# One layer of a hybrid encoder on one core: sums of squares used two products later, two operand pools of the second stage in the other order, and the second stage's last block with fewer merges and one PSUM tile for each last result

## The chip, the cores and the metric

The kernel runs on one core of one Trainium2 chip. The metric is the device time of one execution in microseconds. The five engines each work through their own queue in order: TensorE (PE, matrix products into PSUM), VectorE (DVE), ScalarE (ACT), GpSimd (POOL) and SyncE (SP, which here only issues transfers). ACT issues some transfers too. Shown below are the kernel's times in plain runs and one execution taken by the hardware profiler.

## The reference, cut to what matters

For one batch of 1024 positions of width 1024:

- `u = RMSNorm(x)`, one projection `u @ w_in`, then two mixers side by side: banded attention in chunks of 64, and a gated delta-rule recurrence in chunks.
- `h = x + concat[RMSNorm(attention), delta] @ w_out`
- `h = h + relu(RMSNorm(h) @ w_ff1)^2 @ w_ff2`, with `w_ff1` 1024 x 4096 and `w_ff2` 4096 x 1024, all float32.

The change lies in the last line alone. RMSNorm divides each position by the root of the mean of its squares over 1024 channels; the kernel multiplies the gain in first, squares after the relu, and so needs `1/mean(h*h)` (no root) as a factor on the squared result, one number for each position.

## The kernel before, in words

Everything is kept transposed: channels on the 128 partitions, positions along the free axis, in two halves of 512. A float32 product is made from three float32r products (high x high, high x low, low x high), so each operand is split on the way: ACT copies it to the high part (line 146), DVE subtracts that from it to get the low part (line 147). A page is a 128 x 1024 float32 tile, 4 KB in each partition.

**Stage 1 (`ff1`, lines 987 to 1132)** computes the first product in 8 blocks of 512 hidden channels. Each block is one step of a fast matrix multiplication with 7 products instead of 8, named q1, q2, q5, q6, q3, q7, q4 in the order of the code, of 24 matmuls each. Their position-side operands (b11, b21, t1, t2, b22, t3, t4: quarters of `h` or differences of them) are split once, by `uop`, in the first block and stay in their pools (`ub11` ... `ut4`, four pages each) for all blocks. The four results of a block are z11 (from q1 and q2), z12, y5 and y1; each goes through relu and square on ACT (`square`) and through `emit`, in which DVE multiplies by the factor row `r2` and ACT's queue stores it to `f_dr`.

The factor comes from the sums of squares that the stage before left in `sq_dr`. `norm_col` (1025) loads them into a page `acc`, has PE add them up over the partitions (`hcol`, 16 small matmuls), and DVE makes `r_col` of it. `norm_row` (1035) has PE spread that over all partitions (`hrow`), and ACT copies it to `r2`. Blocks are generators that stop at `yield`; lines 1125 to 1132 step them: q1 of block 0 and of block 1, then `norm_col`; q2 of both, then `norm_row`; then the rest of block 0, of block 1, and the other blocks. z11, z12 of blocks 0 and 1 and `acc` are pages of pool `ut4`, in which the four pages of operand t4 lie too; later blocks use other space (`zz`).

**Stage 2 (`ff2`, 1134 to 1292)** multiplies by `w_ff2` in 4 blocks (`kb` 0 to 3) of 1024 hidden channels, again by 7 products a block, p1, p2, p5, p3, p6, p7, p4, of 48 matmuls. `product` (1150) takes two PSUM tiles of two banks out of the four of pool `psw`, and prepares operand pairs 0 and 1 in turn by `prep5`, `prep3`, ... (sums and differences on DVE, in place) and by splitting. Operands are loaded at the top of a block: a11 and b11 into pool `r`, a12, b21 and b22 into pool `r2`, a21, a22 and b12 into pool `rc`. `accumulate` adds a product to one of the pages y1 to y7 (DVE, one input from PSUM). In the last block `merge` adds one y to another (both inputs in SBUF), on POOL (`nc.gpsimd`) or DVE (`nc.vector`), so that y2, y3, y5 and y4 become the four quarters of the output, which `store` and the last loop write out. The last product, p4, is made row by row (`by_rows`): quarter q of the result is complete before the next begins, and is subtracted into y4 and sent at once.

**What sets the order.** The code's order is only a priority. A planner walks a simulated timeline before the program runs and writes each engine's queue from it; on the chip the queue is then run in that order, whatever the real times. A tile's space is reused in its pool when its last user is done. Stage 2's pools (line 1308) are laid out from the same base as stage 1's (1306), one behind the other in the order of the dictionary, so a page of stage 2 waits for the page of stage 1 that lay there.

Of the kernel before, what the change touches and what calls it, by code (L numbers as in the profile page):

```python
# [8 lines left out]
F32 = mybir.dt.float32  # L9
# [36 lines left out]
def hymba_kernel(  # L46
# [940 lines left out]
    def ff1(R, psw, pools):  # L987
# [2 lines left out]
        B = {}  # L990
        count = [0]
        r2 = pools["r2"][0].tile([P, 2, TH], F32, tag="r2", name="r2", bufs=1)
        begun = {}

        def page2(tag, name, dt=F32):
            pool, n = pools[tag]
# [46 lines left out]
        def block(sb):  # L1043
            def lw(tag, name, kh, c):
                t = page2(tag, f"{name}_{sb}")
                c0 = sb * FB + c * 256
                nc.sync.dma_start(out=t.rearrange("p (k c) -> p k c", k=4),
                                  in_=w_ff1[kh * 512:(kh + 1) * 512, c0:c0 + 256].rearrange("(k p) c -> p k c", p=P))
                return t

            first = "w" if sb else "w0"
            a11 = lw(first, "wa11", 0, 0)
            a12 = lw(first, "wa12", 1, 0)
            if sb > 1:
                a21, a22 = lw("w", "wa21", 0, 1), lw("w", "wa22", 1, 1)
            yy = quarter(f"yy{sb}")
            y1, y5 = wide(yy, 0), wide(yy, 1)

            def product(name, src, key):
                n = f"{name}_{sb}"  # L1060
                ps = psw.tile([P, 1024], F32, tag="bk", name=n)
                ah, al = parts(src, n + "a", key)
                if key in LAST:
                    hi, lo = begun[LAST[key]]
                    with tc.issue_after(hi), tc.issue_after(lo):
                        bop = uop(key)
                else:
                    bop = uop(key)
                for k in range(4):
                    bh, bl = bop[k]  # L1070
                    for q in range(2):
                        s = slice(k * 256 + q * P, k * 256 + (q + 1) * P)
                        for m, (l, r) in enumerate(((ah, bh), (ah, bl), (al, bh))):
                            nc.tensor.matmul(part(ps, q), l[:, s], r, start=(k + m == 0), stop=(k == 3 and m == 2))  # L1074
                return ps

            def square(t):
                nc.scalar.activation(t, t, AF.Relu)
                nc.scalar.activation(t, t, AF.Square)

            def emit(t, fh, th):
                nc.vector.tensor_tensor(two(t), two(t), r2[:, th:th + 1, :].broadcast_to([P, 2, TH]), ALU.mult)
                nc.scalar.dma_start(out=f_dr[sb * 4 + fh * 2:sb * 4 + fh * 2 + 2, :, th * TH:(th + 1) * TH].rearrange(
                    "q p t -> p q t"), in_=two(t))

            ps = product("q1", a11, "b11")
            nc.scalar.copy(y1, ps)
            yield
            ps = product("q2", a12, "b21")
            zz = None  # L1090
            if sb > 1:
                zz = quarter(f"zz{sb}")
            z11 = wide(zz, 0) if zz is not None else page2("ut4", f"z11_{sb}")
            nc.vector.tensor_tensor(z11, y1, ps, ALU.add)
            square(z11)
            yield
            emit(z11, 0, 0)
            if sb <= 1:
                a21, a22 = lw("w", "wa21", 0, 1), lw("w", "wa22", 1, 1)
            s1 = page2("w", f"ws1_{sb}")  # L1100
            nc.vector.tensor_tensor(s1, a21, a22, ALU.add)
            ps = product("q5", s1, "t1")
            nc.scalar.copy(y5, ps)
            nc.vector.tensor_tensor(s1, s1, a11, ALU.subtract)
            ps = product("q6", s1, "t2")
            nc.vector.tensor_tensor(y1, y1, ps, ALU.add)
            nc.vector.tensor_tensor(y5, y5, y1, ALU.add)
            nc.vector.tensor_tensor(a12, a12, s1, ALU.subtract)
            ps = product("q3", a12, "b22")
            z12 = wide(zz, 1) if zz is not None else page2("ut4", f"z12_{sb}")  # L1110
            nc.vector.tensor_tensor(z12, y5, ps, ALU.add)
            square(z12)
            emit(z12, 0, 1)
            nc.vector.tensor_tensor(a21, a11, a21, ALU.subtract)
            ps = product("q7", a21, "t3")
            nc.vector.tensor_tensor(y1, y1, ps, ALU.add)
            nc.vector.tensor_tensor(y5, y5, ps, ALU.add)
            square(y5)
            emit(y5, 1, 1)
            ps = product("q4", a22, "t4")  # L1120
            nc.vector.tensor_tensor(y1, y1, ps, ALU.subtract)
            square(y1)
            emit(y1, 1, 0)

        first = [block(sb) for sb in range(2)]
        for i in range(2):
            for g in first:
                next(g)
            (norm_row if i else norm_col)()
        for g in first + [block(sb) for sb in range(2, DFF // FB)]:  # L1130
            for _ in g:
                pass
# [1 line left out]
    def ff2(psw, pools):  # L1134
# [15 lines left out]
        def product(name, prep, by_rows=False):  # L1150
            t = "AB"[side[0]]
            side[0] ^= 1
            ps = [psw.tile([P, 1024], F32, tag="bk", name=f"{name}{m}") for m in range(2)]
            def step(i, k, q):
                (ah, al), (bh, bl) = ops[i]
                s = slice(k * 512 + q * P, k * 512 + (q + 1) * P)
                for m, (l, r) in enumerate(((ah, bh), (ah, bl), (al, bh))):
                    nc.tensor.matmul(part(ps[q // 2], q % 2), l[:, s], part(r, k),  # L1158
                                     start=(i + k + m == 0), stop=(i + k + m == 4))

            ops = []
            for i in range(2):
                ab = []
                for o, src in zip("ab", prep(i)):
                    hi = page2("h" + t, f"{name}{o}{i}_h", F32R)
                    lo = page2("l" + t, f"{name}{o}{i}_l", F32R)
                    split(src, hi, lo, nc.scalar, nc.vector)
                    ab.append((hi, lo))
                ops.append(ab)
                if not by_rows:  # L1170
                    for k in range(2):
                        for q in range(4):
                            step(i, k, q)
            if by_rows:
                for q in range(4):
                    for i in range(2):
                        for k in range(2):
                            step(i, k, q)
            return ps

        def store(x, j, hf):
            for m in range(2):
                nc.sync.dma_start(out=out[0, (4 * j + 2 * m) * P:(4 * j + 2 * m + 2) * P, hf * TH:(hf + 1) * TH].rearrange(
                    "(q p) t -> p q t", p=P), in_=two(x[m]))

        nb = DFF // (2 * NK * P)
        for kb in range(nb):
# [69 lines left out]
            if last:  # L1257
                merge(nc.gpsimd, 2, 1)
                store(y[2], 0, 0)
                merge(nc.gpsimd, 6, 1)  # L1260
            accumulate(5, product(f"p5{kb}", prep5))
            if last:
                merge(nc.gpsimd, 3, 5)
                for m in range(2):
                    nc.gpsimd.tensor_tensor(y[5][m], y[5][m], h11[m], ALU.add)
            accumulate(3, product(f"p3{kb}", prep3))
            ps = product(f"p6{kb}", prep6)
            if last:
                merge(nc.vector, 7, 6)
                merge(nc.vector, 3, 6)  # L1270
                accumulate(3, ps)
                store(y[3], 0, 1)
                accumulate(7, ps)
                merge(nc.vector, 4, 7)
                merge(nc.gpsimd, 5, 7)
            else:
                accumulate(6, ps)
            ps = product(f"p7{kb}", prep7)
            if last:
                accumulate(4, ps)  # L1280
                accumulate(5, ps)
                store(y[5], 1, 1)
            else:
                accumulate(7, ps)
            ps = product(f"p4{kb}", prep4, last)
            if not last:
                accumulate(4, ps, ALU.subtract)
                continue
            for q in range(4):
                t = part(y[4][q // 2], q % 2)  # L1290
                tt(t, t, part(ps[q // 2], q % 2), ALU.subtract)
                (nc.scalar if q % 2 else nc.sync).dma_start(out=out[0, (4 + q) * P:(5 + q) * P, 0:TH], in_=t)

    def ffn(R):
        with ExitStack() as st:
# [9 lines left out]
            with ExitStack() as st1:  # L1305
                ff1(R, psw, stage(st1, "ff1", {"w0": 2, "h": 2, "l": 2, "ub11": 4, "ub21": 4, "ut1": 4, "ut2": 4,
                                               "ub22": 4, "ut3": 4, "ut4": 4, "w": 6, "h2": 1, "l2": 1, "r2": 1}))
            ff2(psw, stage(st, "ff2", {"s1": 2, "hB": 4, "r": 8, "hA": 4, "lA": 4, "rc": 6, "r2": 8, "lB": 4, "y7": 2}))

    def first_steps(gen, n):  # L1310
        for _ in range(n):
# [77 lines left out]
```

## Time and profile before

| | us |
|---|---|
| median of 3 runs | 1318.98 |
| lowest and highest of them | 1316.98, 1319.04 |
| the profiled execution, whole | 1311.28 |
| its span, first to last instruction | 1309.2 |
| PE busy in it | 1267.2 (97%) |
| DVE busy | 937.3 (72%) |
| ACT busy | 554.3 (42%) |
| POOL busy | 306.0 (23%) |

The profiled execution is 7.7 us shorter than the median of the plain runs. Stage 1 runs from 670 to 984 us of the span, stage 2 from 984 to the end. A busy PE counts matmuls whose ends are modelled, and says nothing of the clock that they ran at; the granted clock stands in a row of its own on the page and in a column of the views by stretches.

### The profile page before, as it was taken

To read this page: it belongs to the slowest core of one execution; us is meant where nothing else is said; L and a number is where in the kernel's file an instruction comes from. 1 tells how busy PE (TensorE), PEld (TensorE's weight loads), DVE (VectorE), ACT (ScalarE), POOL (GpSimd) and SP (SyncE) were. 2 spreads that over 40 slices of the span, in tenths; PEclk is the share of its full clock that TensorE was granted. 3 is DMA by queue.
4 is the path that set the end of the run, shared out by engine and by line. 5 is a ranking of instruction groups with operands and counts; after the bars stand their busy time and mean duration, and the time that the engine had idled before them with its cause. 6 is when DMAs were issued, how large, how long until landed. Compare 5 with 4: busy or idle time off the path is not lost.

```text
span 1309.2 us, 18076 instructions
## 1 busy us (share of the span) xinstructions
PE 1267.2 (97%) x6702; PEld 1044.5 (80%) x6702; DVE 937.3 (72%) x1395; ACT 554.3 (42%) x919; POOL 306.0 (23%) x509
## 2 busy tenths in 40 slices
PE   9999999999999998989999999999998999999997
PEld 7778878788888877868878888888886888888876
DVE  7899978655056565853539767677669878897998
ACT  7323232223266564744345444544445543333330
POOL 4426451543033365533210000000000000000251
PEclk9999999999999999989999999999998999999999
DMA  6214354665573532124341323323288514332002
GB/s 219 65 49 141 95 151 129 137 161 145 197 223 105 166 96 74 53 62 157 129 145 65 113 97 113 129 97 113 80 294 300 181 52 153 98 97 97 1 33 97
DMA packets 129256, 160.65 MB, mean 123 GB/s; under 512 B 22800, under 2 KB 71952, under 8 KB 128656
## 3 DMA queue, kind: packets, MB, share of 16 engines
q1 hardware_dynamic: 111328, 137.73, 34.1%
q10 hardware_dynamic: 17840, 21.76, 4.8%
q8 instruction: 53, 0.87, 0.3%
q14 instruction: 35, 0.29, 0.1%
HBM read 111.75 MB, written 47.71 MB: 122 GB/s over the span
## 4 chain that ended last, share of the span: by engine, by line
PE 73%; DVE 8%; DMA 3%; ACT 2%; POOL 1%; issue 1%; SPq 0%; DVEq 0%; ACTq 0%; POOLq 0%
PE q L1074 23%; PE p L1158 19%; PE op L165 5%; PE av_ps L165 3%; PE aq_ps L165 3%; PE t_o L858 3%; PE g_ps L165 3%; PE ak_ps L165 2%; DVE y L1223 1%; PE t_tpb L837 1%; PE t_tpa L848 1%; PE t_sb L785 1%; PE t_sa L785 1%; DMA t_q<-q_dr 1%; PE t_sb L786 1%
## 5 line engine op out<-in xcount | busy, mean ns | idle before, releaser
L1227 POOL TENSOR_TENSOR y<-y,y 128x1024 f32<-128x1024 f32 x8 | 24.7, 3111 | 587.7 <-DVE y L1223 587.7
L801 DVE CUSTOM_DVE_ANT_0 t_pb<-t_sb,biasn 128x256 f32<-128x256 f32 (+1 forms) x64 | 25.7, 403 | 55.5 <-PE t_sb L786 30.3
L1223 DVE TENSOR_TENSOR y<-y,p 128x1024 f32<-128x1024 f32 x50 | 59.9, 1216 | 5.3 <-PE p L1158 4.4
L165 PE MATMUL op<-mh,wo_h 128*128 128x512 f32 x128 | 50.3, 393 | 0.8 <-ACT wo_h L146 0.5
L165 PE MATMUL op<-ml,wo_h 128*128 128x512 f32 x128 | 50.1, 391 | 0.0
L165 PE MATMUL op<-mh,wo_l 128*128 128x512 f32 x128 | 48.3, 392 | 0.0
L816 ACT ACTIVATE t_pb<-t_pb,t_nm 128x256 f32<-128x256 f32 (+1 forms) x64 | 31.6, 494 | 22.8 <-DVE t_nm L810 15.0
L955 DVE TENSOR_TENSOR h<-op,op_x 128x512 f32<-128x512 f32 x16 | 10.8, 688 | 31.9 <-PE op L165 31.9
L858 PE MATMUL t_o<-t_ta,vt 128*64 128x128 f32 x240 | 29.0, 294 | 1.8 <-DVE t_ta L851 1.1
L962 POOL TENSOR_TENSOR op_q<-op_q 128x512 f32<-128x512 f32 x14 | 19.6, 1397 | 47.5 <-ACT op_q L961 47.3
L810 DVE CUSTOM_DVE_ANT_0 t_pa<-t_sa,biaso,t_nm 128x384 f32<-128x384 f32 (+2 forms) x48 | 26.3, 548 | 5.5 <-PE t_sa L786 3.3
L165 PEld LDWEIGHTS op<-mh,wo_h 128*128 128x128 f32 x128 | 24.0, 188 | 7.0 <-ACT wo_h L146 1.0
L165 PEld LDWEIGHTS op<-mh,wo_l 128*128 128x128 f32 x128 | 24.0, 188 | 5.2 <-issue 0.2
L165 PEld LDWEIGHTS op<-ml,wo_h 128*128 128x128 f32 x128 | 24.0, 188 | 5.0
L819 ACT ACTIVATE t_pa<-t_pa,t_nm 128x384 f32<-128x384 f32 (+2 forms) x48 | 26.4, 550 | 0.1
L165 PE MATMUL g_ps<-uh,wg_h 128*128 128x512 f32 x64 | 25.2, 394 | 1.2 <-ACT wg_h L146 1.2
L848 PE MATMUL t_tpa<-ident,t_pa 128*128 128x128 f32 x120 | 21.7, 285 | 4.5 <-ACT t_on L886 3.2
L785 PE MATMUL t_sb<-ks,t_q 128*128 128x256 f32 (+1 forms) x72 | 23.2, 333 | 2.9 <-DMA t_q<-q_dr 2.9
L165 PE MATMUL g_ps<-uh,wg_l 128*128 128x512 f32 x64 | 25.2, 394 | 0.4 <-POOL wg_l L147 0.4
L165 PE MATMUL dq_ps<-uh,wdq_h 128*128 128x512 f32 x64 | 25.5, 398 | 0.0
L165 PE MATMUL dv_ps<-uh,wdv_l 128*128 128x512 f32 x64 | 25.4, 397 | 0.0
L165 PE MATMUL aq_ps<-waq_h,uh 128*128 128x512 f32 x64 | 25.3, 401 | 0.0
(1106 smaller groups left out, 4418.4 us busy)
## 6 DMA issues: line engine op xcount, KB each, us to landing
wa<-in_w_ff_dram SPq DMA_DIRECT2D x32, 512.0 KB
a<-in_w_ff_dram SPq DMA_DIRECT2D x32, 512.0 KB
b<-f_dr SPq DMA_DIRECT2D x32, 512.0 KB
t_q<-q_dr SPq DMA_DIRECT2D x32, 256.0 KB
f_dr<-yy ACTq DMA_DIRECT2D x16, 512.0 KB
f_dr<-zz ACTq DMA_DIRECT2D x12, 512.0 KB
ks<-k_dr SPq DMA_DIRECT2D x16, 256.0 KB
wo_r<-in_w_out_dram SPq DMA_DIRECT2D x16, 256.0 KB
```

The source lines that it names most:

```text
L165: nc.tensor.matmul(ps, a, b, start=(i == 0), stop=(i == n - 1))
L785: nc.tensor.matmul(o, q[:, i * P:(i + 1) * P], k[:, c], start=True, stop=False)
L801: nc.vector.tensor_tensor_reduce(sb[:, c], bk[:, c], new[g][pp][:, c], -1.0, 3.0e38, ALU.add, ALU.min, nm[:, 4 + i:5 + i])
L810: nc.vector.tensor_tensor_reduce(sa[e][:, 0:wa], bk[:, 0:wa], old[g][i][:, 384 - wa:384], -1.0, nm[:, 4 + i:5 + i], ALU.add, ALU.min, nm[: ...
L816: nc.scalar.activation(sb[:, c], sb[:, c], AF.Exp, bias=m, scale=-1.0, accum_out=T["sums"][:, 4 + i:5 + i])
L819: nc.scalar.activation(sa[e][:, 0:wa], sa[e][:, 0:wa], AF.Exp, bias=m, scale=-1.0, accum_out=T["sums"][:, i:i + 1])
L848: nc.tensor.transpose(tp[:, js], sa[e][:, js], ident)
L858: nc.tensor.matmul(po[64 * e:64 * e + 64, pp * P:(pp + 1) * P], vt[k0 + j][:, 64 * h:64 * h + 64], (ta[e] if j < na else tb)[:, c:c + P], ...
L1074: nc.tensor.matmul(part(ps, q), l[:, s], r, start=(k + m == 0), stop=(k == 3 and m == 2))
L1158: nc.tensor.matmul(part(ps[q // 2], q % 2), l[:, s], part(r, k), start=(i + k + m == 0), stop=(i + k + m == 4))
L1223: nc.vector.tensor_tensor(y[i][m], y[i][m], ps[m], op)
L1227: eng.tensor_tensor(y[i][m], y[i][m], y[z][m], ALU.add)
```

## The change

It has four parts. (1) In stage 1 the generators of the first two blocks are stepped through q1 and q2 of both before `norm_col`, then block 0 through q5 and q6 before `norm_row`; `emit` of z11 of blocks 0 and 1 is put behind `norm_row`. Two `yield`s are added for it. (2) In the dictionary of stage 2's pools `r2` and `rc` change places. (3) In the last block the merge of y1 into y6 goes from POOL to DVE and behind p6, p6 is added to y6 alone and p7 to y7 alone, each then merged on, and y5 gets its last part by a POOL merge; its store goes to ACT's queue. (4) p4 in the last block gets four PSUM tiles, one for each quarter, and its four last transfers all go to SP.

```diff
@@ ff1
-        begun = {}
+        begun, held = {}, []
...
             square(z11)
+            if sb <= 1:
+                held.append((emit, z11))
             yield
-            emit(z11, 0, 0)
             if sb <= 1:
                 a21, a22 = lw("w", "wa21", 0, 1), lw("w", "wa22", 1, 1)
             s1 = page2("w", f"ws1_{sb}")
             nc.vector.tensor_tensor(s1, a21, a22, ALU.add)
             ps = product("q5", s1, "t1")
             nc.scalar.copy(y5, ps)
+            yield
+            if sb > 1:
+                emit(z11, 0, 0)
             nc.vector.tensor_tensor(s1, s1, a11, ALU.subtract)
             ps = product("q6", s1, "t2")
             nc.vector.tensor_tensor(y1, y1, ps, ALU.add)
             nc.vector.tensor_tensor(y5, y5, y1, ALU.add)
+            yield
...
         for i in range(2):
             for g in first:
                 next(g)
-            (norm_row if i else norm_col)()
+        norm_col()
+        for _ in range(2):
+            next(first[0])
+        norm_row()
+        for emit, z in held:
+            emit(z, 0, 0)
@@ ff2, product and store
-            ps = [psw.tile([P, 1024], F32, tag="bk", name=f"{name}{m}") for m in range(2)]
+            ps = [psw.tile([P, 1024], F32, tag="bk", name=f"{name}{m}") for m in range(4 if by_rows else 2)]
...
-                    nc.tensor.matmul(part(ps[q // 2], q % 2), l[:, s], part(r, k),
+                    nc.tensor.matmul(part(ps[q], 0) if by_rows else part(ps[q // 2], q % 2), l[:, s], part(r, k),
...
-        def store(x, j, hf):
+        def store(x, j, hf, eng=nc.sync):
             for m in range(2):
-                nc.sync.dma_start(
+                eng.dma_start(
@@ ff2, the blocks
             if last:
                 merge(nc.gpsimd, 2, 1)
                 store(y[2], 0, 0)
-                merge(nc.gpsimd, 6, 1)
             accumulate(5, product(f"p5{kb}", prep5))
+            accumulate(3, product(f"p3{kb}", prep3))
+            accumulate(6, product(f"p6{kb}", prep6))
             if last:
+                merge(nc.vector, 6, 1)
                 merge(nc.gpsimd, 3, 5)
                 for m in range(2):
                     nc.gpsimd.tensor_tensor(y[5][m], y[5][m], h11[m], ALU.add)
-            accumulate(3, product(f"p3{kb}", prep3))
-            ps = product(f"p6{kb}", prep6)
+                merge(nc.vector, 3, 6)
+                store(y[3], 0, 1)
+            accumulate(7, product(f"p7{kb}", prep7))
             if last:
                 merge(nc.vector, 7, 6)
-                merge(nc.vector, 3, 6)
-                accumulate(3, ps)
-                store(y[3], 0, 1)
-                accumulate(7, ps)
                 merge(nc.vector, 4, 7)
                 merge(nc.gpsimd, 5, 7)
-            else:
-                accumulate(6, ps)
-            ps = product(f"p7{kb}", prep7)
-            if last:
-                accumulate(4, ps)
-                accumulate(5, ps)
-                store(y[5], 1, 1)
-            else:
-                accumulate(7, ps)
+                store(y[5], 1, 1, nc.scalar)
             ps = product(f"p4{kb}", prep4, last)
             if not last:
                 accumulate(4, ps, ALU.subtract)
                 continue
             for q in range(4):
                 t = part(y[4][q // 2], q % 2)
-                tt(t, t, part(ps[q // 2], q % 2), ALU.subtract)
-                (nc.scalar if q % 2 else nc.sync).dma_start(out=out[0, (4 + q) * P:(5 + q) * P, 0:TH], in_=t)
+                tt(t, t, part(ps[q], 0), ALU.subtract)
+                nc.sync.dma_start(out=out[0, (4 + q) * P:(5 + q) * P, 0:TH], in_=t)
@@ ffn
-  {"s1": 2, "hB": 4, "r": 8, "hA": 4, "lA": 4, "rc": 6, "r2": 8, "lB": 4, "y7": 2}
+  {"s1": 2, "hB": 4, "r": 8, "hA": 4, "lA": 4, "r2": 8, "rc": 6, "lB": 4, "y7": 2}
```

## Rows read from the trace of the kernel before

**Rows 1.** The page: busy time of the engines over the whole span, and the chain that ended last by engine.

```profile
PE 1267.2 (97%) x6702; PEld 1044.5 (80%) x6702; DVE 937.3 (72%) x1395; ACT 554.3 (42%) x919; POOL 306.0 (23%) x509
...
PE 73%; DVE 8%; DMA 3%; ACT 2%; POOL 1%; issue 1%; SPq 0%; DVEq 0%; ACTq 0%; POOLq 0%
```

**Rows 2.** Who waited for whom, PE alone, whole span: us in total, times, the longest; the rows of stages 1 and 2.

```profile
PE p L1158 <- ACT p20b_h L146: 5.4, 1, 5.4
...
PE p L1158 <- DVE p43b_l L147: 2.5, 1, 2.5
PE hcol L1031 <- DMA acc<-sq_dr: 2.2, 1, 2.2
...
PE p L1158 <- DVE y L1223: 2.0, 1, 2.0
```

**Rows 3.** PE in order of time around `hcol` (start, duration, idle before and its releaser in brackets), and the stretch 685 to 690 us (busy time and instructions of PE, PEld, DVE, ACT, POOL; granted clock; DMA share; GB/s).

```profile
681.91 0.39 PE L1074 MATMUL q<-b11h,q_1a_l 128*128 128x512 f32 x1
684.51 1.92 PE L1031 MATMUL hcol<-ones,acc 128*128 128x1 f32 x16 [2.21 <-DMA acc<-sq_dr]
686.29 0.48 PE L1074 MATMUL q<-b21h,q_0a_h 128*128 128x512 f32 x1
...
690.95 0.40 PE L1074 MATMUL q<-b21l,q_0a_h 128*128 128x512 f32 x1
...
685.00:690.00 5.00, 5.00 (x24) 4.24 (x25) 5.00 (x5) 2.98 (x4) 0.00 (x0) 0.74 0.00 0
```

**Rows 4.** Two stretches with the columns of rows 3: 695 to 700 us, and the last product of the third block of stage 2 (its 48 matmuls and the one under way); and two subtractions of DVE in order of time.

```profile
695.00:700.00 5.00, 5.00 (x29) 4.30 (x28) 5.00 (x6) 3.58 (x4) 0.00 (x0) 1.00 0.07 15
...
1209.13:1220.01 10.88, 10.88 (x49) 9.01 (x48) 10.85 (x10) 4.01 (x5) 0.00 (x0) 1.00 0.00 0
...
700.48 1.23 DVE L147 TENSOR_TENSOR t2l<-h,t2h 128x1024 fp32r<-128x1024 f32 x1
...
720.10 1.22 DVE L147 TENSOR_TENSOR t4l<-h,t4h 128x1024 fp32r<-128x1024 f32 x1
```

**Rows 5.** Where stage 1 ends and stage 2 begins, in order of time on PE, ACT, DVE and SP; one row of SP's waits; the stretch 990 to 1000 us with the columns of rows 3.

```profile
1000.06 1.22 PE L1158 MATMUL p<-p20b_h,p20a_h 128*128 128x512 f32 x2 [5.38 <-ACT p20b_h L146]
...
1004.88 0.39 PE L1158 MATMUL p<-p50b_h,p50a_h 128*128 128x512 f32 x1
...
1000.85 1.06 ACT L146 CAST p20b_h<-b 128x1024 fp32r<-128x1024 f32 x1
...
981.80 1.22 DVE L1111 TENSOR_TENSOR z<-yy,q 128x1024 f32<-128x1024 f32 x1
...
986.38 1.22 DVE L1233 TENSOR_TENSOR s<-a,a 128x1024 f32<-128x1024 f32 x1
...
978.17 1.40 SPq L1193 DMA_DIRECT2D a<-in_w_ff_dram  x3
979.61 1.34 SPq L1193 DMA_DIRECT2D b<-f_dr  x2
...
995.71 0.89 SPq L1193 DMA_DIRECT2D b<-f_dr  x2
...
SPq L1193 <- DMA f_dr<-z: 8.2, 1, 8.2
...
990.00:1000.00 10.00, 4.68 (x21) 3.56 (x19) 10.00 (x9) 7.70 (x9) 0.00 (x0) 0.90 1.03 377
```

**Rows 6.** The last block in order of time: POOL, then DVE, then PE.

```profile
1249.27 5.75 POOL L1227 TENSOR_TENSOR y<-y,y 128x1024 f32<-128x1024 f32 x2 [10.24 <-DVE y L1223]
1260.72 6.63 POOL L1227 TENSOR_TENSOR y<-y,y 128x1024 f32<-128x1024 f32 x2 [5.70 <-DVE y L1223]
1267.31 6.72 POOL L1265 TENSOR_TENSOR y<-y,h 128x1024 f32<-128x1024 f32 x2
1286.60 5.72 POOL L1227 TENSOR_TENSOR y<-y,y 128x1024 f32<-128x1024 f32 x2 [12.56 <-DVE y L1223]
...
1244.57 1.21 DVE L1227 TENSOR_TENSOR y<-y,y 128x1024 f32<-128x1024 f32 x1
...
1250.24 2.51 DVE L1239 TENSOR_TENSOR a<-a,s 128x1024 f32<-128x1024 f32 x1
1252.67 3.44 DVE L1252 TENSOR_TENSOR b<-b,b 128x1024 f32<-128x1024 f32 x1
...
1284.11 4.61 DVE L1223 TENSOR_TENSOR y<-y,p 128x1024 f32<-128x1024 f32 x4
...
1300.11 1.28 DVE L1291 TENSOR_TENSOR y<-y,p 128x512 f32<-128x512 f32 x2
...
1260.70 0.71 PE L1158 MATMUL p<-p63b_h,p63a_h 128*128 128x512 f32 x1 [1.99 <-DVE y L1223]
...
1264.18 0.42 PE L1158 MATMUL p<-p63b_h,p63a_l 128*128 128x512 f32 x1
...
1293.45 0.50 PE L1158 MATMUL p<-p43b_l,p43a_h 128*128 128x512 f32 x1 [2.55 <-DVE p43b_l L147]
...
1298.61 0.40 PE L1158 MATMUL p<-p43b_l,p43a_h 128*128 128x512 f32 x1
```

**Rows 7.** The end: DVE, SP, and the end of the chain that ended last.

```profile
1304.77 1.29 DVE L1291 TENSOR_TENSOR y<-y,p 128x512 f32<-128x512 f32 x2 [3.38 <-PE p L1158]
...
1300.22 0.37 SPq L1183 DMA_DIRECT2D out_dram<-y  x1
```

More of the change, by code (lines that the diff above doesn't have):

```diff
@@ L1179, in product @@
             return ps
-        def store(x, j, hf):
+        def store(x, j, hf, eng=nc.sync):
             for m in range(2):
-                nc.sync.dma_start(out=out[0, (4 * j + 2 * m) * P:(4 * j + 2 * m + 2) * P, hf * TH:(hf + 1) * TH].rearrange(
+                eng.dma_start(out=out[0, (4 * j + 2 * m) * P:(4 * j + 2 * m + 2) * P, hf * TH:(hf + 1) * TH].rearrange(
                     "(q p) t -> p q t", p=P), in_=two(x[m]))
@@ L1307, in ffn @@
                                                "ub22": 4, "ut3": 4, "ut4": 4, "w": 6, "h2": 1, "l2": 1, "r2": 1}))
-            ff2(psw, stage(st, "ff2", {"s1": 2, "hB": 4, "r": 8, "hA": 4, "lA": 4, "rc": 6, "r2": 8, "lB": 4, "y7": 2}))
+            ff2(psw, stage(st, "ff2", {"s1": 2, "hB": 4, "r": 8, "hA": 4, "lA": 4, "r2": 8, "rc": 6, "lB": 4, "y7": 2}))
     def first_steps(gen, n):
```

## The prediction

> **What bounds the kernel now.** First the page: PE is busy for 1267.2 of 1309.2 us, and the chain that ended last runs through PE for 73% of the span [rows 1]. So time is saved where PE waits, or runs at its lower clock after a wait. The second view is who waited for whom, PE alone [rows 2]. Four waits lie where the change reaches: 2.2 us for the sums of squares, 5.4 us at the start of p2 in stage 2, and 2.0 and 2.5 us in the last block. The third is PE in order of time. At full speed 48 matmuls start in 10.88 us, 0.227 us each [rows 4]. After the wait at `hcol`, 13 matmuls take from 686.29 to 690.95, 4.66 us instead of 2.95 (1.7 lost), and the granted clock of the stretch is 0.74, a mean of the levels 1.2 and 2.4 GHz [rows 3]. After the 5.38 us wait 11 matmuls take 1000.06 to 1004.88: 4.82 instead of 2.50, 2.3 lost [rows 5]. In the last block 8 take 1260.70 to 1264.18 (1.7 lost) and 15 take 1293.45 to 1298.61 (1.8 lost) [rows 6]. A wait thus costs its own length and about 2 us more:
>
> - sums of squares 2.2 + 1.7 = 3.9
> - start of p2 5.4 + 2.3 = 7.7
> - last block 2.0 + 1.7 + 2.5 + 1.8 = 8.0
>
> Together 19.6 us; add a short tail behind PE's last matmul.
>
> **Part 1, sums of squares later.** `hcol` waits because `acc` lands at 684.5, while q1 of block 1 has started its last matmul at 681.91 [rows 3]. Put behind the two q2 (2 x 24 x 0.227 = 10.9 us), it comes at 693 and finds `acc` there. The q2 started directly behind `hcol`, so its operands were ready: 2.2 us of waiting go. The 1.7 us of low clock go with them unless `hcol` alone brings it down; `hrow`, 16 matmuls as well, stands in 695 to 700 at a granted 1.00 [rows 4]. Added are no instructions; the two `emit` and the load of `acc` keep their queues. Late next is DVE, which is full: 5.00 of 5.00 us both in 685 to 690 and in 695 to 700 [rows 3, 4]. PE would reach q6 at about 693 + 1.9 + 5.4 = 700.3 and want the second half of t2 2.7 us later, at 703.0; its low part ends at 701.7 now [rows 4], and z11, now ready sooner, goes ahead of it once (1.2 us): 702.9, in time by a hair. Further on t4's first low part ends at 721.3, and PE arrives up to 3.9 us earlier than it did. Bounds: all 3.9 gained if DVE's order gives way, 0.5 if DVE holds PE back for nearly all of it. I take 3.0.
>
> **Part 2, the pools change places.** Counted in pages from the base, stage 1 has ub22 at 22 to 25, ut3 at 26 to 29, ut4 at 30 to 33, then w. `r2` lies on 28 to 35 before and 22 to 29 after, `rc` on 22 to 27 and then 30 to 35. So p2's operands (a12, b21) now wait for t3, t4 and the page that z12 of block 1 took when t4 left it; that sum is made only at 981.80, its store must land, SP waits 8.2 us for that, and the load of b21's last page goes out at 995.71 [rows 5]. Because they come late, ACT's queue has p2's casts behind p5's, and PE waits. After, a12 and b21 lie on pages that are free when q3 and q7 are done, at 978.2 at the latest, which is when `rc`'s loads went out before. Those were in SBUF when DVE added two of them at 986.38 [rows 5]; a cast (1.05) and a subtraction (1.22) later, at 989, p2 could go, and p1 ends at 1000.06 - 5.38 = 994.7. So 7.7 us go. Late next is p5, whose operands take over the pages of t4. The page behind z12's store is free at 995.71; b21's second page, loaded then, was cast at 1000.85, so 5.1 us bound load and queue. A sum (1.22), a cast and a subtraction bring 1004.3; p2 ends at 994.7 + 10.9 = 1005.6. That is 1.3 us of slack, with DVE full (10.00 of 10.00) and the DMA share at 1.03 [rows 5]. Bounds: 7.7 gained, or 1.0 if p5 takes over most of the wait. I take 6.7.
>
> **Parts 3 and 4, the last block.** A two-input operation of DVE on SBUF takes 1.2 us alone and 3.4 beside POOL; one with an input in PSUM keeps 1.15 (4.61 for four, half beside POOL); POOL's take 2.9 to 3.4 each [rows 6]. From 1250.24 to 1301.39 DVE does 32 whole operations and 2 halves in 51.2 us, from the first of the rows with that start to the last [rows 6]: 32 x 1.135 + 1.2 = 37.5 of work, so the eight POOL operations cost it 13.6, or 1.7 each. It is this backlog that makes PE wait both times. The change takes away:
>
> - the POOL pair at 1249.27, which slowed the two operations from 1250.24 to 1256.1: 2 x 1.7 = 3.4;
> - two DVE operations: before 16 accumulations (beside the last four halves) and 6 merges, after 12 and 8: 2 x 1.135 = 2.3. (Two of the merges, y6 into y7, were done by 1245.8 [rows 6] and now come behind p7.)
>
> DVE would come to the second half at 1301.4 - 5.7 = 1295.7; PE without waits ends at 1304.75 - 8.0 = 1296.8. But a chain now begins with p7's end (1296.8 - 10.9 = 1285.9): y7 gets p7 (2), y6 is merged in (2), y4 gets y7 (2), while POOL adds y7 to y5 (2). That is 6 x 1.135 + 2 x 1.7 = 10.2, to 1296.1; then four halves at 0.6, to 1298.5. The last half ended at 1304.77 + 1.29 = 1306.06 [rows 7]: 7.5 gained. The PSUM tile for each quarter frees q2 from waiting for q3 (0.6, inside that sum). Against it, y5's last store went out at 1300.22, 5.8 us before the last half [rows 7]; now its pages come with y4's, 2 MB in the last few us, and the tail of 3.1 us may grow; I take 1.2 of 0 to 2. ACT issues nothing else then, so the queue that the store moves to costs nothing. Gained: 7.5 - 1.2 = 6.3; bounds 8.6 (tail too) and 1.7 (only the wait at p6 goes, 3.7, and y5 is 2 late).
>
> The Trainium skill (SBUF — State Buffer, section Who interferes with whom) says that a VectorE operation with at most one SBUF input does not contend with GpSimd and one with two does, the later of the two being blocked whole. The rows agree. It speaks against this part: p7 went into y4 and y5 by accumulations with one SBUF input, and goes now by two-input merges beside POOL; by the rule alone each of the two merges into y4 waits for a whole POOL operation, some 2 us more than I reckon.
>
> **Sum.** 3.0 + 6.7 + 6.3 = 16.0. From the profiled execution's 1311.3 that makes 1295.3; its median stands 7.7 us higher in the plain runs, and I carry the difference over: 1318.98 - 16.0 = 1303.0.
>
> **The rivals.**
>
> 1. The last block stays bound by what DVE and POOL share: the merges behind p7 keep DVE past PE's end, and only the wait at p6 is won. For it speaks that DVE was busy for 10.85 of 10.88 us already in the product before [rows 4], against it the 5.7 us of work removed. 1318.98 - 3.0 - 6.7 - 1.7 = 1307.6.
> 2. p5 takes the wait over: the page behind z12's store, or the loads behind it in SP's queue, come 5 us late. For it the DMA share of 1.03, against it the 1.3 us of slack and a queue that carries the same bytes. 1318.98 - 3.0 - 1.0 - 6.3 = 1308.7.
> 3. Slower: the planner leaves PE's queue as it is, two matmuls of p2, then 31 of p5 (they run from 1001.08), then the rest of p2. p5's operands are now the late ones. If all six loads go out from 995.7 on at 377 GB/s, 0.52 MB take 1.4 us each and the last is in at 1004; one pair's four operations on DVE and a cast make it 1009.6, and six more of DVE's in front 1016.4. PE then waits 21.7 us and loses 2.3, 24.0 instead of 7.7: 16.3 lost against 9.3 gained elsewhere, 1326. It decides when p5's operands come later than 994.7 + 5.4 + 9.3 = 1009.4. Against it: p2's operands are ready first by 6 us, and the planner goes by that.
> 4. The sums of squares are not used later, because the planner issues `hcol` where it was: part 1 is worth nothing, 1306.
>
> **Chances.** The forecast 0.50, rival 1 0.22, rival 2 0.12, rival 3 0.07, rival 4 0.09. About 0.2%, 2.6 us, is what a measurement of this kernel can tell from no change. Two of rivals 1, 2 and 4 together, with part 1 lost to DVE, would come near no change: 0.06 out of their 0.43. So faster 0.87, same 0.06, slower 0.07. The range goes from 1297 (all upper bounds, 20.2, with 2 us of scatter) to 1313 (rivals 1 and 2 at once: 3.0 + 1.0 + 1.7 = 5.7).
>
> **What would show it.** `hcol` behind two q2, with no wait of PE and a granted clock of 1.0 around it; p1, p2, p5 in this order with less than 1.5 us between them; no wait of PE for an accumulation before p6; POOL with eight operations instead of ten from 1225 on; the last half of y4 some 2 us behind PE's last matmul. A new wait of PE at q6, t4, p5 or p4's second pair would each show one of my terms wrong; one above 5 us would make the prediction wrong.

## The result, and the profile after

| | before | after |
|---|---|---|
| median of 18 plain runs each, on one chip (us) | 1316.69 | 1307.92 |
| the profiled execution, whole (us) | 1311.28 | 1307.01 |
| its span (us) | 1309.2 | 1305.2 |

The ratio is 0.9943 with a 95% interval of 0.9925 to 0.9961: 7.5 us faster (5.1 to 9.9). The forecast was 16.0 us. The time lies inside the range given, but less than half of the gain came.

To see where, I cut the span at the starts of certain products on PE, which do the same work in both kernels: from the first q1 to q1 of block 2 (the sums of squares lie in it), from p1 of stage 2's first block to p1 of the second (the pools), and from p5 of the last block to PE's last matmul. The view by stretches, PE alone; columns: stretch, its length, PE busy with its matmuls, granted clock, DMA share, GB/s. Before:

```profile
671.17:755.16 83.99, 81.78 (x368) 0.98 0.35 117
983.64:1067.69 84.05, 78.67 (x337) 0.96 0.58 196
1241.77:1304.73 62.96, 58.42 (x241) 0.95 0.15 59
```

After:

```profile
673.19:754.97 81.78, 80.12 (x368) 1.00 0.35 120
983.45:1071.40 87.95, 79.71 (x338) 0.94 0.53 183
1245.48:1300.04 54.56, 54.56 (x241) 1.00 0.14 51
```

The first stretch gained 2.2 us, the second lost 3.9, the third gained 8.4. What lies between them (754.97 to 983.45, 1071.40 to 1245.48) has the same length in both to 0.01 us, and from PE's last matmul to the end of the span it is 5.2 instead of 4.5. That is 6.0 us gained. The span shows 4.0, because the first q1 starts 2.0 us later, ahead of everything that the change touches. Over all profiles of this study that start lies between 671.2 and 680.2, and it goes with PE's clock in the stage before: from 400 to 600 us the granted clock is 0.98 in the kernel before, 0.97 in the changed one and 0.93 in the profile with 680.2 (e2). Why the clock differs there is open.

PE's waits in the changed kernel, us in total, times, longest; they answer to [rows 2]:

```profile
PE p L1168 <- ACT p50b_h L146: 4.5, 1, 4.5
PE p L1168 <- DVE p50b_l L147: 3.8, 1, 3.8
...
PE hrow L1039 <- DVE r_col L1033: 1.7, 1, 1.7
```

(Most lines of `ff2` are 10 higher than before: `product` multiplies in 1168, loads are 1203, `accumulate` is 1233, `merge` 1237.) All four waits of [rows 2] are gone: for `hcol`, p20b, p43b and the accumulation. Three others have come. **The one that matters is p5's.** In order of time, PE, then SP, then DVE, then ACT; they answer to [rows 5]:

```profile
994.33 0.39 PE L1168 MATMUL p<-p20b_h,p20a_h 128*128 128x512 f32 x1
...
1009.85 0.83 PE L1168 MATMUL p<-p50b_h,p50a_h 128*128 128x512 f32 x2 [4.47 <-ACT p50b_h L146]
1014.44 0.79 PE L1168 MATMUL p<-p50b_l,p50a_h 128*128 128x512 f32 x1 [3.76 <-DVE p50b_l L147]
...
978.20 0.88 SPq L1203 DMA_DIRECT2D b<-f_dr  x2
991.47 3.06 SPq L1203 DMA_DIRECT2D a<-in_w_ff_dram  x4
994.57 5.16 SPq L1203 DMA_DIRECT2D b<-f_dr  x4
...
1001.69 1.22 DVE L1243 TENSOR_TENSOR s<-a,a 128x1024 f32<-128x1024 f32 x1 [7.47 <-DMA a<-in_w_ff_dram]
...
1008.75 1.04 ACT L146 CAST p50b_h<-b 128x1024 fp32r<-128x1024 f32 x1 [4.75 <-DVE b L1244]
```

p2 starts at 994.33 directly behind p1, as forecast. But from 979.08 (978.20 + 0.88) to 991.47 SP issues nothing, and then all of p5's loads in one go: four of `a` (a21, a22) and the first two of `b` (b12). One row of SP's waits, and two pieces of the chain that ended last (start, length):

```profile
SPq L1203 <- DMA f_dr<-z: 12.2, 1, 12.2
```

```profile
988.58 2.75 DMA f_dr<-z
993.53 8.13 DMA a<-in_w_ff_dram
```

SP waits 12.2 us for the store of z12 of block 1. The third load, issued at 993.53, lands 8.1 us later, for all six share the way with each other and with stage 1's last stores: from 1000 to 1010 the DMA share is 1.04. DVE stands idle for 7.5 us until that load is in, and then has the sums for p5 among others to do. The same view, all engines (PE, PEld, DVE, ACT, POOL, clock, DMA share, GB/s):

```profile
990.00:1000.00 10.00, 10.00 (x46) 8.26 (x44) 4.22 (x4) 4.50 (x5) 0.00 (x0) 1.00 0.79 256
1000.00:1010.00 10.00, 5.53 (x25) 4.29 (x24) 8.28 (x8) 2.31 (x3) 0.00 (x0) 1.00 1.04 396
1010.00:1020.00 10.00, 6.24 (x15) 4.54 (x16) 10.00 (x10) 3.78 (x4) 0.00 (x0) 0.52 0.21 65
```

Why the store stands in the way of those loads: pages of stage 2 lie on pages of stage 1. The profile doesn't name pages; counted from the code as in the prediction, the first load for p5, of a21, is given page 30. z12 of block 1 is on page 30 too, because part 1 of the change has z11 ask for a page of `ut4` ahead of `acc`, so that the four pages are dealt out otherwise; before, z12 of block 1 had page 33. So the load at the head of six waits for the last user of its page, and SP works in order. e2 and e5 below test this count.

**The last block**, POOL, DVE and ACT's transfers in order of time; they answer to [rows 6, 7]:

```profile
1247.45 6.62 POOL L1237 TENSOR_TENSOR y<-y,y 128x1024 f32<-128x1024 f32 x2 [572.24 <-DVE y L1233]
1267.43 5.75 POOL L1237 TENSOR_TENSOR y<-y,y 128x1024 f32<-128x1024 f32 x2 [13.36 <-issue]
1273.13 6.75 POOL L1277 TENSOR_TENSOR y<-y,h 128x1024 f32<-128x1024 f32 x2
1293.57 7.85 POOL L1237 TENSOR_TENSOR y<-y,y 128x1024 f32<-128x1024 f32 x2 [13.70 <-DVE y L1237]
...
1292.22 4.62 DVE L1237 TENSOR_TENSOR y<-y,y 128x1024 f32<-128x1024 f32 x4
1296.76 1.87 DVE L1292 TENSOR_TENSOR y<-y,p 128x512 f32<-128x512 f32 x3
1300.08 0.69 DVE L1292 TENSOR_TENSOR y<-y,p 128x512 f32<-128x512 f32 x1 [1.45 <-PE p L1168]
...
1299.13 2.71 ACTq L1193 DMA_DIRECT2D out_dram<-y  x2
```

POOL has eight operations, PE none of its waits, and the last half waits for PE instead of the other way round. **The sums of squares**, PE:

```profile
695.04 1.84 PE L1031 MATMUL hcol<-ones,acc 128*128 128x1 f32 x16
...
709.58 2.02 PE L1039 MATMUL hrow<-ident,r_col 128*128 128x128 f32 x16 [1.65 <-DVE r_col L1033]
```

And DVE's two steps to `r_col`:

```profile
704.63 0.15 DVE L1032 TENSOR_SCALAR r_col<-hcol 128x8 f32<-128x8 f32 x1
...
709.24 0.19 DVE L1033 RECIPROCAL r_col<-r_col 128x8 f32<-128x8 f32 x1
```

`hcol` runs without a wait and the granted clock of the whole stretch is 1.00, so sixteen small matmuls did not bring it down. `hrow` now waits 1.65 us: `hcol` is done at 696.9, but the two short steps stand behind whole-page operations in DVE's queue.

### The profile page after: what moved, and what is told of

Read it like the earlier page. It is cut to its first block, busy times and chain, and to the rows that moved or that the text cites. A ratio compares the mean times of both kernels' runs of the same rounds, so it can differ in the third digit from the quotient of the medians.

```text
span 1305.2 us, 18066 instructions
## 1 busy us (share of the span) xinstructions
PE 1267.1 (97%) x6702; PEld 1045.7 (80%) x6702; DVE 929.1 (71%) x1393; ACT 554.6 (42%) x919; POOL 301.3 (23%) x507
## 4 chain that ended last, share of the span: by engine, by line
PE 72%; DVE 7%; DMA 3%; issue 2%; ACT 2%; POOL 1%; POOLq 1%; SPq 0%; ACTq 0%; DVEq 0%
PE q L1074 21%; PE p L1168 19%; PE op L165 5%; PE av_ps L165 3%; PE aq_ps L165 3%; PE t_o L858 3%; PE g_ps L165 3%; PE ak_ps L165 2%; PE t_tpb L837 1%; PE t_tpa L848 1%; PE t_sb L785 1%; PE t_sa L785 1%; DMA t_q<-q_dr 1%; PE c_po L460 1%; DMA a<-in_w_ff_dram 1%
## 5 line engine op out<-in xcount | busy, mean ns | idle before, releaser
L1237 POOL TENSOR_TENSOR y<-y,y 128x1024 f32<-128x1024 f32 x6 | 20.2, 3388 | 599.3 <-DVE y L1233 572.2
L1233 DVE TENSOR_TENSOR y<-y,p 128x1024 f32<-128x1024 f32 x46 | 55.3, 1213 | 3.0 <-PE p L1168 2.4
L858 PEld LDWEIGHTS t_o<-t_ta,vt 128*64 128x64 f32 x240 | 17.8, 143 | 9.4 <-issue 1.9
```

The lines of the kernel that those rows point to most:

```text
L858: nc.tensor.matmul(po[64 * e:64 * e + 64, pp * P:(pp + 1) * P], vt[k0 + j][:, 64 * h:64 * h + 64], (ta[e] if j < na else tb)[:, c:c + P], ...
L1233: nc.vector.tensor_tensor(y[i][m], y[i][m], ps[m], op)
L1237: eng.tensor_tensor(y[i][m], y[i][m], y[z][m], ALU.add)
```

## The experiments

Each run was compared with the kernel before on one chip. For each kernel the lengths of the three stretches and of the tail (PE's last matmul to the span's end) in its profile, their sum against the profile of before, and the plain runs (ratio times the median of before in that comparison):

| run | sums of squares | pools | last block | tail | sum, us | plain runs: ratio (95%) | us |
|---|---|---|---|---|---|---|---|
| before | 83.99 | 84.05 | 62.96 | 4.46 | | | |
| changed | 81.78 | 87.95 | 54.56 | 5.17 | -6.0 | 0.9943 (0.9925 to 0.9961) | -7.5 |
| e1 | 81.83 | 84.08 | 54.56 | 5.20 | -9.8 | 0.9939 (0.9916 to 0.9962) | -8.0 |
| e2 | 83.97 | 80.20 | 61.27 | 4.45 | -5.6 | 0.9996 (0.9975 to 1.0017) | -0.5 |
| e3 | 81.80 | 84.34 | 61.27 | 4.46 | -3.6 | 0.9985 (0.9967 to 1.0002) | -2.0 |
| e4 | 85.57 | 84.08 | 54.56 | 5.20 | -6.1 | 0.9942 (0.9923 to 0.9962) | -7.6 |
| e5 | 81.81 | 80.07 | 54.57 | 5.18 | -13.8 | 0.9884 (0.9864 to 0.9904) | -15.3 |
| e6 | 81.81 | 82.40 | 54.56 | 5.20 | -11.5 | 0.9903 (0.9883 to 0.9923) | -12.8 |
| e7 | 84.26 | 83.86 | 63.45 | 3.86 | 0.0 | 0.9992 (0.9978 to 1.0006) | -1.1 |
| e8 | 81.84 | 80.43 | 54.56 | 5.57 | -13.1 | 0.9888 (0.9869 to 0.9906) | -14.7 |
| e9 | 81.85 | 83.37 | 54.56 | 5.19 | -10.5 | 0.9902 (0.9880 to 0.9924) | -12.9 |
| e10 | 87.35 | 83.18 | 54.57 | 5.19 | -5.2 | 0.9970 (0.9948 to 0.9991) | -3.9 |
| e11 | 81.83 | 76.16 | 54.56 | 5.20 | -17.7 | 0.9862 (0.9846 to 0.9879) | -18.2 |

The stretches carry the plain runs within their intervals in all but e2. The unchanged last block shows 62.96 and 61.27, with the same waits of 2.0 and 2.5 us. The 1.7 us lie behind the second wait: in the kernel before PE then ran at low clock [rows 6], in e2 and e3 it didn't. Of e3, PE, and the stretch behind the wait with the columns of rows 3:

```profile
1293.72 0.50 PE L1168 MATMUL p<-p43b_l,p43a_h 128*128 128x512 f32 x1 [2.50 <-DVE p43b_l L147]
...
1294.00:1298.00 4.00, 4.00 (x19) 3.27 (x19) 4.00 (x4) 0.00 (x0) 0.00 (x0) 1.00 0.01 4
```

**e1 to e4: each part by itself.** e1 is the changed kernel with the pools back in place, e2 the kernel before with the pools changed:

```diff
-"r2": 8, "rc": 6, "lB": 4
+"rc": 6, "r2": 8, "lB": 4
```

(e2 the other way round.) e3 takes over `ff1` alone, e4 `ff2` alone, from the changed kernel.

> The changed kernel with the two pools back in their old places. Theory A (the page of z12 of block 1): what waits in stage 2 is whatever load has the page that z12 of block 1 took, and all that is queued behind it on SP, because z12's store lands only at about 995. With the sums of squares later, that page is page 30 instead of 33, and in the old order of the pools no load of stage 2's first block uses page 30; so p2 loses its wait of 5.4 us, p5 has none, and the time is 2.2 + 7.7 + 7.7 = 17.6 us under before: ratio 0.987. Theory B (the area): the pages that t4 held are late because they come free only when stage 1's last product is done, store or no store; then p2 waits some 5 us as before, and the time is 2.2 + 7.7 = 9.9 us under before: ratio 0.9925.

Measured: p2 waits exactly as before. The first row is PE's wait; then two of SP's rows, ACT's, in order of time:

```profile
PE p L1168 <- ACT p20b_h L146: 5.4, 1, 5.4
```

```profile
989.54 2.77 SPq L1203 DMA_DIRECT2D b<-f_dr  x2
...
999.59 1.05 ACT L146 CAST p50b_h<-b 128x1024 fp32r<-128x1024 f32 x1
1000.54 1.05 ACT L146 CAST p20a_h<-a 128x1024 fp32r<-128x1024 f32 x1
...
1003.38 1.05 ACT L146 CAST p20b_h<-b 128x1024 fp32r<-128x1024 f32 x1
```

Theory A falls for p2: its last two loads go out from 989.54 on, the last at 991.94, 5.8 us behind p1's start (986.16), where it was 995.71, 12.1 behind [rows 5]; that changes nothing. p2's casts stand behind p5's in ACT's queue, where the planner put them. Theory B's number came out, for another reason than B's; so a third theory (C, the planner's order) had to be tried, in e6.

> The kernel before with the pools' places changed and nothing else. Here z12 of block 1 has page 33, which becomes that of a221, the fourth of the six loads for p5. Theory A: a221 and the two loads of b12 behind it go out at about 995.7 as in the changed kernel, p2 runs without a wait, and p5 waits 4 to 8 us and runs some us at low clock: between no change and 4 us slower, ratio 1.000 to 1.003. Theory B: the loads go out at about 984 when t4 has been read, p5 has its operands by 1000, and 6.7 us are gained: ratio 0.995.

Measured: the block took 80.20, so the change of the pools by itself gained 3.9 us there, where in the changed kernel it lost 3.9. The plain runs don't show the gain (0.9996; the lower end, 0.9975, is 3.3 us). They scatter from 1308.5 to 1321.0 us; I leave open what the whole time is worth, and use the stretch. SP's rows, and PE's wait:

```profile
990.14 1.40 SPq L1193 DMA_DIRECT2D a<-in_w_ff_dram  x3
...
1001.76 0.37 SPq L1193 DMA_DIRECT2D a<-in_w_ff_dram  x1
1002.22 1.54 SPq L1193 DMA_DIRECT2D b<-f_dr  x3
```

```profile
PE p L1158 <- DVE p50b_l L147: 2.0, 1, 2.0
```

Here z12 of block 1 has page 33, the fourth load's. Three of the six go out ahead of the wait, the rest 9.1 us after p1's start (992.67) instead of 8.0 as in the changed kernel, and still p5 waits only 2.0 us. So it is not that a load waits for the store, but that the first one does and five stand behind it. The expected loss was mine: A priced every place in the queue alike.

> The kernel before with the sums of squares used later and nothing else. Theory A: besides the 2.2 us in stage 1, p2's wait (7.7 us with its low clock) goes, since z12 of block 1 moves to page 30, which no load of stage 2's first block uses: 9.9 us gained, ratio 0.9925. Theory B: 2.2 us gained, p2 still waits 5 us: ratio 0.998.

Measured: 2.2 us in its stretch, none in the pools' (84.34), ratio 0.9985. A falls here as in e1.

> The kernel before with the two edits of the last block and nothing else. Both theories: PE has no wait for an accumulation after 1250 and stage 2's start is as before (p2 waits 5.4 us): 7.7 us gained, ratio 0.994. If the last block's gain in the changed kernel came from PE's arriving there later, it is under 4 us, ratio over 0.997.

Measured: 0.9942, PE without a wait after 1250. The last block's gain stands by itself. (`hcol`'s wait cost 1.6 us more in this profile, by the clock: 0.96 in that stretch.)

**e5: the page.** The changed kernel with the page of z12 of block 1 under y7, which nothing loads:

```diff
-"r2": 8, "rc": 6, "lB": 4, "y7": 2
+"r2": 8, "y7": 2, "rc": 6, "lB": 4
```

> The changed kernel with y7 and rc one place apart: y7 takes pages 30 and 31, rc 32 to 37, lB 38 to 41, so that the page of z12 of block 1 (30) belongs to y7, which is written only at the end of p7. Stage 2's first block (start of p1 to start of the next p1) took 84.05 us before and 87.95 in the changed kernel; seven products without a wait take 76.2. Theory A (in the new order of the pools, p5 waits because the first of its loads has the page of z12 of block 1, and the other five stand behind it in SP's queue): the loads go out by about 985, p5 has its operands before p2 ends, the block takes 76 to 79 us, the time is 9 to 12 us under the changed kernel's: ratio to before 0.985 to 0.988. Theory B (the pages of t4 and w are late by themselves, with a DMA share near 1): p5 still waits 3 us or more, the block takes 82 to 86: ratio 0.990 to 0.993.

Measured: 80.07 instead of 87.95, ratio 0.9884: 7.9 us out of one place in a dictionary. SP and DVE:

```profile
984.03 1.99 SPq L1203 DMA_DIRECT2D a<-in_w_ff_dram  x4
...
1001.91 1.22 DVE L1257 TENSOR_TENSOR a<-a,a 128x1024 f32<-128x1024 f32 x1
1003.04 1.22 DVE L1244 TENSOR_TENSOR b<-b,b 128x1024 f32<-128x1024 f32 x1
1004.18 1.22 DVE L1248 TENSOR_TENSOR s<-s,a 128x1024 f32<-128x1024 f32 x1
1005.32 1.22 DVE L1244 TENSOR_TENSOR b<-b,b 128x1024 f32<-128x1024 f32 x1
1007.15 2.58 DVE L1233 TENSOR_TENSOR y<-y,p 128x1024 f32<-128x1024 f32 x2 [0.62 <-PE p L1168]
1009.65 1.22 DVE L147 TENSOR_TENSOR p50b_l<-b,p50b_h 128x1024 fp32r<-128x1024 f32 x1
```

The four `a` loads go out 2.5 us before p1 starts (986.55), and SP's wait of 12.2 us is gone. (All six pages of `rc` move up by two with this edit, not the first alone.) A holds for p5, though the block missed its 76 to 79 us, and B falls. It gained less than A's 9 to 12: 2.0 us of wait are left, the same in e2, and they are DVE's: p5's second low part stands behind sums that p7 (1257) and p3 (1248) need much later, and behind p2's accumulation.

**e6: the planner's order.** e1, with p5's splits in the first block held behind p2's last ones:

```diff
-accumulate(5, product(f"p5{kb}", prep5))
+accumulate(5, product(f"p5{kb}", prep5, behind=tuple(casts) if kb == 0 else ()))
...
```

> The kernel of the first run (old order of the pools), with p5's casts and low parts in the first block put behind p2's on ACT and DVE. There p2's loads all went out by 992, its four casts stood behind p5's four on ACT, at 1000.5 to 1004.4, and p2 waited 5.4 us. Theory C (that wait is the planner's order of ACT's queue, no load): p2's casts come at about 994 to 998, p2 waits under 1.5 us, the first block takes 76 to 80 us instead of 84.1, 4 to 8 us under the first run: ratio to before 0.988 to 0.991. Theory B (p2's pages and loads are late): p2 waits 4 us or more, ratio 0.994.

Measured: 82.40 instead of 84.08, ratio 0.9903; p2 waits 3.35 and 0.71 us instead of 5.38. ACT:

```profile
998.77 1.01 ACT L1236 COPY y<-p 128x1024 f32<-128x1024 f32 x1 [0.34 <-PE p L1170]
999.63 0.37 ACTq L1083 DMA_DIRECT2D f_dr<-yy  x1
1000.04 1.04 ACT L146 CAST p20a_h<-a 128x1024 fp32r<-128x1024 f32 x1 [0.26 <-issue]
```

C holds in part: the order took 1.3 us off the wait and 1.7 off the block, but p2's casts still stand behind p1's copies, as in e1, where these began at 995.88 and 998.69, and so they begin 1.3 us behind p1's end (998.74). That p2 could have gone without a wait in the old order of the pools was not shown.

**e7 and e8: the end.** e7 is the kernel before with four PSUM tiles for p4's quarters; e8 is e5 with the last merge on DVE:

```diff
-merge(nc.gpsimd, 5, 7)
+merge(nc.vector, 5, 7)
```

> The kernel before with nothing but a PSUM tile for each last result. My sum: 0.6 us at most at the very end, both PE waits of the last block stay (2.0 and 2.5 us): ratio 0.999 to 1.000. Rival: that the halves of y4 wait for a whole PSUM tile is what keeps the end late, and 2 us or more go: ratio 0.998 or less.

> The kernel of run e5 with the last merge, y7 into y5, on DVE instead of POOL. In the changed kernel that POOL pair takes 7.85 us and ends at about 1301.4, 1.4 us behind PE, and PE's end to the span's end is 5.2 us (4.5 before). If POOL's pair sets the end: DVE does it in 2.3 us and its neighbours, alone now, faster; y5 goes out some 2 us earlier and 1 to 2 us of the end go, ratio 0.001 under e5's. If DVE's queue sets the end: the last four halves come 2 us later, ratio 0.001 to 0.002 over e5's.

Measured: e7 0.9992, no difference that can be measured, and both waits stayed, the second with 4.1 us instead of 2.5. Behind the first PE ran at full clock here (1.00 from 1266 to 1270), came sooner, and waited for the same low part: it starts 51.68 us behind p5's start in e7 as in the kernel before, e2 and e3. So DVE's queue sets that moment. e8 0.9888 beside e5's 0.9884: the same. Without POOL, y5's pages go out 2.3 us sooner, counted from PE's end, but DVE comes to the halves of y4 2.3 us later and SP then issues all four in a row (1294.57 to 1297.1). Neither theory of e8 was right. My reading is that the bytes of y5 and y4 together hold the end: the DMA share is 1.00 from 1296 to 1298 in e8, and 1.01 to 1.02 from 1299 to 1303 in the changed kernel.

**e9 to e11: what is left of p5's wait, and `hrow`.** On e5, in the first block alone. e9 holds the sums of p7 and p3 behind p5's low parts and p2's accumulation behind its first; e11 holds only p7's sums, behind p3's low parts, and p2's accumulation. Of e11:

```diff
+with ExitStack() as st:
+    if kb == 0:
+        st.enter_context(tc.issue_after(casts["p30", "b", 1]))
     tt(a21[i], a11[i], a21[i], ALU.subtract)
     tt(b12[i], b22[i], b12[i], ALU.subtract)
...
+with tc.issue_after(casts["p50", "b", 0]):
+    accumulate(2, ps)
```

e10 is e9 with one more `next(first[1])` ahead of `norm_row()`.

> The kernel of run e5, where p5 still waits 2.0 us for its second low part, with DVE's order changed in stage 2's first block: the sums that only p3, p6 and p7 need (three instructions) and the accumulation of p2 (two) come behind p5's low parts. Theory D (what is left of the wait is DVE's order): p50b's low part lands some 3 us sooner, before p2 ends; the wait (2.0) and its low clock (1.9) go, the first block takes 76 to 77.5 us instead of 80.07: ratio to before 0.985 to 0.986 where e5 had 0.9884. Theory E (DVE is full there, so what is put behind is missed next): p3 or p6 waits as much, the block takes 79 us or more, ratio 0.988 or more.

> The kernel of run e9 with hrow behind one product more (q5 of block 1). In the changed kernel PE waits 1.65 us at hrow for r_col, which stands late in DVE's queue; the stretch from the first q1 to q1 of block 2 takes 81.8 us (84.0 before). If the wait hangs on hrow's place alone: it goes, the stretch takes 80.1, 1.7 us or 0.0013 of the ratio under e9's. If DVE is behind anyway: PE waits the same 1 to 2 us at a later product, ratio as e9's.

> The kernel of run e5 with DVE's order changed less than in e9: in stage 2's first block p7's four sums come behind p3's low parts and p2's accumulation behind p5's first low parts; the sums for p3 and p6 stay where the planner puts them. Theory D (what is left of the wait is DVE's order, and e9 only put the wrong sums back): p5 and p3 start without a wait, the first block takes 76 to 78 us instead of 80.07: ratio to before 0.985 to 0.987. Theory E (DVE has no room at all in this block): a wait of 2 us or more turns up at p5's second pair, p3, p6 or p7, the block takes 79 us or more: ratio 0.988 or more.

Measured: in e9 p5 starts without a wait, and p3 pays more than was saved:

```profile
PE p L1170 <- ACT p30b_h L146: 4.9, 1, 4.9
```

The block took 83.37. In e10 PE had to take q5 of block 1 first, whose cast was not ready, and `hrow` came 41.6 us behind the first q1 (719.23) where it was 36.4 in the changed kernel; the stretch went from 81.85 to 87.35:

```profile
718.21 0.80 PE L1074 MATMUL q<-t1h,q_1a_h 128*128 128x512 f32 x1 [5.79 <-ACT q_1a_h L146]
```

By the stretches both are losses. In e11 only the sums with time to spare were put back, and the block is without a wait, at full clock, its 336 matmuls at 0.227 us each:

```profile
988.28:1064.44 76.16, 76.16 (x337) 1.00 0.61 212
```

Ratio 0.9862, 18.2 us under the kernel before: the best version of this study, and, each taken against the kernel before, 10.7 us under the changed kernel. Theory D holds, E falls: DVE had room, if the right instructions gave way (p7's four sums and p2's two accumulations).

## Why the prediction was right or wrong

**Part 1: the mechanism was right, 2.2 us instead of 3.0.** `hcol` stands behind two q2, its wait and the low clock behind it are gone (3.9). "Late next is DVE" was right, the place was not: t2's second low part was in time, and `r_col`, two short steps that DVE's queue has at 704.63 and 709.24, made `hrow` wait 1.65. 3.9 - 1.65 = 2.2. e3 shows the part alone. What the prediction left out: the part changes which page z12 of block 1 gets, and that cost more than it gained.

**Part 2: the failed step.** It reads: "The page behind z12's store is free at 995.71; b21's second page, loaded then, was cast at 1000.85, so 5.1 us bound load and queue." That is the price of one load with few behind it. Here the load that waits is the first of six, and its page I had taken as it was before part 1. The page came free earlier than I reckoned (the loads went out from 991.47), and p5 was still 4.5 and then 3.8 us late, since the third load needed 8.1 us, and four operations of DVE lie between the first sum and the difference that p5's cast waits for, four more ahead of the low part. e5 against the changed kernel shows that the page at the head of the queue is worth 7.9 us; e2 shows that the same wait at the fourth place leaves 2.0 us of wait. The lower bound, 1.0 us gained, was wrong as well: nothing in the rows excluded a loss, and 3.9 were lost. This is rival 2, in place and mechanism, at the wrong price. The right price stood under rival 3: six loads at once, DVE's operations and a cast, "make it 1009.6"; p5 started at 1009.85. That they agree so closely is luck: the loads went out 4.2 us sooner than in that sum, and DVE's operations took 2.5 us longer (7.0 from 1001.69, where 4.5 were reckoned). I had tied that sum to an order of PE's queue that did not come (p2 went first), and had not carried it over to rival 2, where p2's end at 1005.4 makes 4.5 us of it. The sign that the prediction set for itself, a new wait above 5 us, was met by neither wait alone; the two together are 8.2.

Why p2 waited before was half right. Its casts stand behind p5's on ACT, as read, but not because its loads come late on the chip: in e1 the last goes out 5.8 us behind p1's start instead of 12.1, and p2 waits 5.4 us all the same.

**Parts 3 and 4: right, 7.7 us instead of 6.3** in the profiles (6.0 against the unchanged last block of 61.27). Against p5's start in the block, the last half ends 9.0 us sooner (1306.06 - 1241.77 = 64.29; 1300.77 - 1245.48 = 55.29) where 7.5 were reckoned; from there to the end it is 1.3 us longer, where 1.2 were. e4 shows the parts alone, e7 that part 4 gives nothing by itself. One term was mis-read: the 1.7 us of low clock behind the first wait were no price of their own, for DVE's queue sets when p43b's low part comes (51.68 us behind p5's start, with low clock there or without, e7). And the 1.8 us behind the second wait came in the kernel before, but not in e2 and e3; hence 7.7 or 6.0. Rival 1 falls: PE has no wait after 1240 though DVE stays busy. The rule of the Trainium skill (SBUF — State Buffer, section Who interferes with whom), as the prediction read it, would have made the merges into y4 wait some 2 us for POOL. The four two-input merges (into y7 and y4) took 4.62 us, 1.15 each, which is their time alone; POOL's pair, begun 1.35 us after DVE's four, took 7.85 where such a pair took 5.75 and 6.62 earlier in the block. In kind that agrees with the rule, the later of the two was held up: but the later was POOL. PE did not wait for it; y5's stores did, the second to 1301.4, but e8, without that pair, was no faster.

**Rivals 3 and 4** fall by the order on PE: `hcol` moved, and p1, p2, p5 came in the order forecast.

**The sum**: 2.2 - 3.9 + 7.7 = 6.0 where 3.0 + 6.7 + 6.3 = 16.0 was forecast; the difference is 10.0, and part 2 alone is 10.6 of it. The time fell into the range because parts 1, 3 and 4 came; part 2 lay outside its own bounds.

## What to carry to other kernels

When pages or pools change places, write down for each load of the next stage whose page it gets and when that user's last transfer lands, and do it again after every other edit that allocates from the same pool; a late page costs most under the first load of an in-order queue. A wait's price is what comes in behind it: count the loads that start together and the operations between the last of them and PE. And read the order of an engine's queue as planned, not as a result of what came late on the chip.

## What was not expected of the hardware

- What a wait of PE cost on top of its length varied. In the pools' stretch, length less 76.16 less the waits is 1.9 us in e5 (wait 2.0), 2.3 in e9 (4.95) and 2.5 in the kernel before (5.38). But 2.50 us in the last block of e3 cost nothing on top, with a granted clock of 1.00 behind it, and neither did 2.0 us in that of e7 nor 1.65 at `hrow`. The prediction's "about 2 us more" is thus no fixed price; what decides it no run here shows.
- The two long waits of the changed kernel, 4.47 and 3.76 with two matmuls between them, cost 11.8 - 8.2 = 3.6 us on top, and the clock from 1010 to 1020 was 0.52, about the lower level of the two (1.2 of 2.4 GHz).
- POOL's merge, begun at 1293.57 beside the second of DVE's four, had its result at 1299.13, when ACT sent it off: the first of its two operations took 5.5 us and the second, when DVE had only PSUM operands left, 2.35. It looks as if the first had waited for three operations of DVE in a row (to 1296.8), not for one, though spans on POOL are rough. Other pairs of that block share the time by turns: 6.62 for POOL's two at 1247.45, and 2.31 and 3.42 for two of DVE's beside them.
- A load of 0.5 MB took 8.1 us to land among the loads that went out with it, where the store of z12, as large, had taken 2.75 just before.
